# Expert combine: one load for the first tile, and the order of two issues on ScalarE's queue

## The chip, the cores and the metric

The kernel runs on one core of one Trainium2 chip. The metric is the device time of one execution in microseconds; lower is better. The profile is of one execution on that core, and its times are counted from the first instruction (the span's start).

## The reference

For each of 16 x 1024 tokens, two experts' outputs of 512 numbers are multiplied by their two weights and added:

```
expert_outputs   [16, 1024, 2, 512] float32
combine_weights  [16, 1024, 2]      float32
out = sum(expert_outputs * combine_weights[..., newaxis], axis=2)   # [16, 1024, 512]
```

In all, 67.1 MB of expert outputs and 0.13 MB of weights are read, and 33.6 MB are written.

## The kernel before

The 16,384 tokens lie over 128 partitions, 128 tokens to each. A token's two expert rows are 4 KB on end, its output 2 KB. The first 115 tokens of each partition (`main`) form one block of the input, the last 13 (`LAST`) another, so that a partition's tokens in a tile are one contiguous row in memory: 13 tokens are 52 KB of input and 26 KB of output.

The tokens go through ten tiles (`TILES`: 13, 13, 12, 13, 13, 13, 12, 13, 13, 13 tokens per partition). The buffer `et` has four rooms (`ROOM`), and tile g uses room g mod 4. Tiles 0 to 3 are loaded at the start, from SyncE's queue (`load`, line 76); `FIRST` gives the sizes of these loads. In the kernel before there are five, as the first tile is cut into 2 and 11 tokens, and the load of the 2 tokens is told to make rows of no more than 4 KB (`max_dma_last_dim`).

`combine` computes in place. For tiles 0 to 7 VectorE multiplies the whole tile by the weights (line 88) and adds the two halves into the room's beginning (line 97). For tile 8 ScalarE does a part (lines 92, 94, 96, 97). Tile 9 goes token by token through ScalarE (line 102) and VectorE (line 103). Each result is stored (line 130) from ScalarE's queue, except the last two stores, which go from SyncE's: that of tiles 7 and 8 together and that of tile 9. When a tile is stored and its store has landed, SyncE loads the tile that uses the room next.

ScalarE's queue issues four small DMAs first: 16 rows of 512 B of zeroes, spread over the output (`ahead`, line 111; the zeroes come from `zt`, which VectorE sets at line 108, and the real output overwrites them later); the weights of the first 115 tokens (`weights`, line 79; 920 B per partition); and the weights of the last 13 in two halves of the partitions (line 114). Then it loads its activation table with a first small activation (line 115).

The order of instructions on each engine is that of the program (`manual_schedule`). The waits between them are put in by the framework, on semaphores; it has eight for DMAs, and a DMA that takes over one of them waits until the DMA that had it has landed. Both queues, SyncE's (q1 in the profile) and ScalarE's (q10), feed the same 16 DMA engines. One row of a transfer is one packet on one engine.

Of the kernel before, what the change touches and what calls it, by code (L numbers as in the profile page):

```python
# [1 line left out]

# [4 lines left out]


@with_exitstack
def kernel(  # L10
    ctx: ExitStack,
    tc: tile.TileContext,
    expert_outputs: bass.AP,
    combine_weights: bass.AP,
    out: bass.AP,
):

    nc = tc.nc
    b, s, k, h = expert_outputs.shape
    assert k == 2
    n = b * s
    P = nc.NUM_PARTITIONS
    per = n // P
    assert per * P == n

    ROOM = [13, 13, 12, 13]
    ROOMS = len(ROOM)  # L30
    SITE = [sum(ROOM[:i]) for i in range(ROOMS)]
    TILES = [13, 13, 12, 13, 13, 13, 12, 13, 13, 13]
    FIRST = [2, 11, 13, 12, 13]
    STORES = [[0], [1], [2], [3], [4], [5], [6], [7, 8], [9]]
    WHOLE = [0, 1, 2, 3, 4, 5, 6, 7]
    MIXED = [8]
    ALONE = 3
    FREE = {9: 0}
    LAST = 13
    assert all(c <= ROOM[g % ROOMS] for g, c in enumerate(TILES))  # L40
    assert sum(TILES) == per and [g for st in STORES for g in st] == list(range(len(TILES)))
    main = per - LAST
    starts = [sum(TILES[:g]) for g in range(len(TILES))]

    def rows(x):

        first = x[0 : P * main, :].rearrange("(p t) f -> p t f", p=P)
        second = x[P * main : n, :].rearrange("(p t) f -> p t f", p=P)
        return lambda t, c: first[:, t : t + c, :] if t < main else second[:, t - main : t - main + c, :]

    flat = out.rearrange("b s h -> (b s) h")
    eo = rows(expert_outputs.rearrange("b s k h -> (b s) (k h)"))
    cw = rows(combine_weights.rearrange("b s k -> (b s) k"))
    o = rows(flat)

    dt = mybir.dt.float32
    mult = mybir.AluOpType.mult
    add = mybir.AluOpType.add
    copy = mybir.ActivationFunctionType.Copy

    pool = ctx.enter_context(tc.tile_pool(name="all", bufs=1))
    et = pool.tile([P, sum(ROOM), k * h], dt)
    halves = et.rearrange("p j (k h) -> p (j k) h", k=k)
    wt = pool.tile([P, per * k], dt)
    wk = wt.rearrange("p (t k) -> p t k", k=k)
    zt = pool.tile([16, 128], dt)
    warm = pool.tile([P, 1], dt)

    def place(t):
        g = max(g for g in range(len(TILES)) if starts[g] <= t)  # L70
        return SITE[g % ROOMS] + t - starts[g]

    def load(t, c, **kw):
        at = place(t)
        assert place(t + c - 1) == at + c - 1
        nc.sync.dma_start(out=et[:, at : at + c], in_=eo(t, c), **kw)  # L76

    def weights(q, t, c):
        q.dma_start(out=wk[:, t : t + c, :], in_=cw(t, c))

    def combine(g, base):
        at, c, t0 = SITE[g % ROOMS], TILES[g], starts[g]
        if g in WHOLE or g in MIXED:
            room = halves[:, k * at : k * (at + c), :]
            x0, x1 = et[:, at : at + c, 0:h], et[:, at : at + c, h : 2 * h]
            if g in WHOLE:
                wb = wt[:, k * t0 : k * (t0 + c)].unsqueeze(2).to_broadcast([P, k * c, h])
                nc.vector.tensor_tensor(out=room, in0=room, in1=wb, op=mult)  # L88
            else:
                for i in range(ALONE, c):  # L90
                    x = et[:, at + i, 0:h]
                    nc.scalar.activation(out=x, in_=x, func=copy, scale=wt[:, k * (t0 + i) : k * (t0 + i) + 1])  # L92
                w1 = wk[:, t0 : t0 + c, 1:2].to_broadcast([P, c, h])
                nc.vector.tensor_tensor(out=x1, in0=x1, in1=w1, op=mult)  # L94
                w0 = wk[:, t0 : t0 + ALONE, 0:1].to_broadcast([P, ALONE, h])
                nc.vector.tensor_tensor(out=x0[:, 0:ALONE], in0=x0[:, 0:ALONE], in1=w0, op=mult)  # L96
            nc.vector.tensor_tensor(out=halves[:, base : base + c, :], in0=x0, in1=x1, op=add)  # L97
            return
        for i in range(c):
            t = k * (t0 + i)  # L100
            x0, x1 = halves[:, k * (at + i), :], halves[:, k * (at + i) + 1, :]
            nc.scalar.activation(out=x0, in_=x0, func=copy, scale=wt[:, t : t + 1])  # L102
            nc.vector.scalar_tensor_tensor(  # L103
                out=halves[:, base + i, :], in0=x1, scalar=wt[:, t + 1 : t + 2], in1=x0, op0=mult, op1=add
            )

    with tc.manual_schedule():
        nc.vector.memset(zt, 0.0)  # L108

        ahead = flat[0 : P * main, :].rearrange("(q t) h -> q (t h)", q=16)  # L110
        nc.scalar.dma_start(out=ahead[:, 0:128], in_=zt)  # L111
        weights(nc.scalar, 0, main)
        for half in (slice(0, P // 2), slice(P // 2, P)):
            nc.scalar.dma_start(out=wk[half, main:per, :], in_=cw(main, per - main)[half])
        nc.scalar.activation(out=warm, in_=nc.const_aps.tensor(1.0, (P, 1), dt), func=copy)  # L115

        t = 0
        for i, c in enumerate(FIRST):
            load(t, c, **({"max_dma_last_dim": k * h * 4} if i == 0 else {}))
            t += c  # L120
        assert t == sum(TILES[:ROOMS])
        for j, st in enumerate(STORES):
            room = FREE.get(st[0], st[0] % ROOMS)
            base, c = SITE[room] * k, 0
            for g in st:
                combine(g, base + c)
                c += TILES[g]
            assert c <= k * ROOM[room]
            q = nc.sync if j in (7, 8) else nc.scalar
            q.dma_start(out=o(starts[st[0]], c), in_=halves[:, base : base + c, :])  # L130
            for g in st:
                if g + ROOMS < len(TILES):
                    load(starts[g + ROOMS], TILES[g + ROOMS])


# [1 line left out]
_INS = ['expert_outputs', 'combine_weights']  # L137
_OUTS = [((16, 1024, 512), 'float32')]


# [23 lines left out]
```

## Time and profile before

| what | value |
|---|---|
| time, median of 3 runs | 238.95 us (238.85 to 239.05) |
| profiled execution, span from first to last instruction | 237.1 us |
| VectorE busy in the span | 190.0 us (80%) |
| ScalarE busy | 15.8 us (7%) |
| moved by DMA | 100.80 MB in 3344 packets, mean 425 GB/s over the span |
| packets of SyncE's queue (q1) | 77.33 MB, 75.9% of the 16 engines' time |
| packets of ScalarE's queue (q10) | 23.47 MB, 23.0% |

The profile gives for the profiled execution its span alone; the runs' times are device times of other executions of the same program and include what lies before and behind the span. In the profile's rows, PE, DVE, ACT, POOL and SP are TensorE, VectorE, ScalarE, GpSimd and SyncE; a q behind a name (SPq, ACTq) is that engine's queue, on which DMAs are issued. `et` is the tile buffer, `wt` the weights, `zt` the zeroes, `out_dram` the output.

### The profile page before, as it was taken

The page shows a single profiled execution, that of the slowest core. Times are in us where ns is not written, and L with a number is a line of the kernel's source. Part 1 is how long each engine was busy: PE and PEld are TensorE (multiplying, and loading weights), DVE is VectorE, ACT ScalarE, POOL GpSimd, SP SyncE. Part 2 cuts the span into 40 slices and gives each one's busy share as a digit, 9 for nine tenths or more (in the row PEclk, how much of TensorE's full clock was granted, in tenths as well). Part 3 has the DMA queues.
Part 4 walks back from the last instruction along what each step waited for, and adds up shares of the span by engine and source line. Part 5 has one row for each costly group of instructions (what it writes and reads, how often), then busy time and mean ns, then how long its engine had stood idle before and what let it go on. Part 6 is the DMA issues. An engine that isn't in the chain of part 4 may idle for free.

```text
span 237.1 us, 154 instructions
## 1 busy us (share of the span) xinstructions
DVE 190.0 (80%) x33; ACT 15.8 (7%) x25; POOL 0.2 (0%) x4
## 2 busy tenths in 40 slices
DVE  0006999999999999999999998998499969919400
ACT  2000000000000000000000000000000055019200
POOL 0000000000000000000000000000000000000000
DMA  8999999989999999999899999999899999899996
GB/s 300 388 481 434 432 421 398 470 348 485 449 431 458 431 440 390 486 420 420 359 492 409 409 509 392 431 503 431 359 431 503 420 397 483 381 431 431 431 431 287
DMA packets 3344, 100.80 MB, mean 425 GB/s; under 512 B 512, under 2 KB 656, under 8 KB 912
## 3 DMA queue, kind: packets, MB, share of 16 engines
q1 hardware_dynamic: 2000, 77.33, 75.9%
q10 hardware_dynamic: 1344, 23.47, 23.0%
HBM read 67.24 MB, written 33.56 MB: 425 GB/s over the span
## 4 chain that ended last, share of the span: by engine, by line
DVE 55%; DMA 36%; issue 1%; ACT 0%; DVEq 0%; ACTq 0%; SPq 0%
DVE et L88 35%; DVE et L97 17%; DMA out_dram<-et 17%; DMA et<-in_expert_outputs_dram 12%; DMA wt<-in_combine_weights_dram 8%; DVE et L103 3%; ACT et L102 0%; DVEq L159 0%; ACTq L111 0%; DVE zt L108 0%; DVEq L88 0%; SPq L76 0%; ACTq L102 0%
## 5 line engine op out<-in xcount | busy, mean ns | idle before, releaser
L88 DVE TENSOR_TENSOR et<-et,wt 128x13312 f32<-128x13312 f32 (+1 forms) x8 | 110.0, 13754 | 23.8 <-DMA wt<-in_combine_weights_dram 18.7
L97 DVE TENSOR_TENSOR et<-et 128x6656 f32<-128x6656 f32 (+1 forms) x9 | 62.8, 6973 | 0.4
L92 ACT ACTIVATE et<-et,wt 128x512 f32<-128x512 f32 x10 | 6.2, 708 | 188.0 <-DMA et<-in_expert_outputs_dram 188.0
L103 DVE SCALAR_TENSOR_TENSOR et<-et,wt 128x512 f32<-128x512 f32 x13 | 8.7, 747 | 5.0 <-ACT et L102 5.0
L102 ACT ACTIVATE et<-et,wt 128x512 f32<-128x512 f32 x13 | 8.1, 707 | 14.0 <-DMA et<-in_expert_outputs_dram 14.0
L94 DVE TENSOR_TENSOR et<-et,wt 128x6656 f32<-128x6656 f32 x1 | 7.1, 7093 | 2.3 <-DMA et<-in_expert_outputs_dram 2.3
L96 DVE TENSOR_TENSOR et<-et,wt 128x1536 f32<-128x1536 f32 x1 | 1.8, 1751 | 0.0
L115 ACT ACT_TABLE_LOAD x1 | 1.3, 1283 | 3.1 <-issue 3.1
L108 DVE MEMSET zt<- 16x128 f32 x1 | 0.2, 165 | 0.8 <-PEq L148 0.8
L115 ACT ACTIVATE warm<-const-float32-1.0 128x1 f32<-128x1 f32 x1 | 0.2, 203 | 0.0
L148 POOL MEMSET const-bfloat16-1.0<- 128x1 bf16 x1 | 0.1, 102 | 0.0
L148 POOL MEMSET const-uint8-127<- 128x1 uint8 x1 | 0.1, 101 | 0.0
L148 POOL MEMSET const-float32-0.0<- 128x1 f32 x1 | 0.1, 99 | 0.2 <-issue 0.2
L148 POOL MEMSET const-float32-1.0<- 128x1 f32 x1 | 0.1, 98 | 0.0
## 6 DMA issues: line engine op xcount, KB each, us to landing
et<-in_expert_outputs_dram SPq DMA_DIRECT2D x7, 6656.0 KB, 32.2
out_dram<-et ACTq DMA_DIRECT2D x5, 3328.0 KB, 34.7
et<-in_expert_outputs_dram SPq DMA_DIRECT2D x2, 6144.0 KB, 41.1
out_dram<-et SPq DMA_DIRECT2D x1, 6656.0 KB, 19.9
out_dram<-et ACTq DMA_DIRECT2D x2, 3072.0 KB, 37.2
et<-in_expert_outputs_dram SPq DMA_DIRECT2D x1, 5632.0 KB, 18.2
out_dram<-et SPq DMA_DIRECT2D x1, 3328.0 KB, 14.0
et<-in_expert_outputs_dram SPq DMA_DIRECT2D x1, 1024.0 KB, 5.0
```

Of the source, the lines that this page charges most:

```text
L88: nc.vector.tensor_tensor(out=room, in0=room, in1=wb, op=mult)
L92: nc.scalar.activation(out=x, in_=x, func=copy, scale=wt[:, k * (t0 + i) : k * (t0 + i) + 1])
L94: nc.vector.tensor_tensor(out=x1, in0=x1, in1=w1, op=mult)
L96: nc.vector.tensor_tensor(out=x0[:, 0:ALONE], in0=x0[:, 0:ALONE], in1=w0, op=mult)
L97: nc.vector.tensor_tensor(out=halves[:, base : base + c, :], in0=x0, in1=x1, op=add)
L102: nc.scalar.activation(out=x0, in_=x0, func=copy, scale=wt[:, t : t + 1])
L103: nc.vector.scalar_tensor_tensor(out=halves[:, base + i, :], in0=x1, scalar=wt[:, t + 1 : t + 2], in1=x0, op0=mult, op1=add)
L108: nc.vector.memset(zt, 0.0)
L115: nc.scalar.activation(out=warm, in_=nc.const_aps.tensor(1.0, (P, 1), dt), func=copy)
L148: nc = _bacc.Bacc("TRN2", target_bir_lowering=False, num_devices=1)
```

## The change

The first tile's 13 tokens are loaded by one DMA, with rows of 52 KB, instead of one of 2 tokens in rows of 4 KB and one of 11 tokens in rows of 44 KB. ScalarE's queue issues the weights of the first 115 tokens first and then the zeroes. In the instruction streams, SyncE has ten loads instead of eleven; ScalarE's first two DMAs change places; the framework's semaphores go round one place earlier, and with them the load of tile 3 takes over the semaphore of the main weights, where it had that of the zeroes. VectorE's instructions are the same, and its first multiply waits for two DMAs instead of three.

```diff
-    FIRST = [2, 11, 13, 12, 13]
+    FIRST = [13, 13, 12, 13]
...
-    def load(t, c, **kw):
+    def load(t, c):
...
-        nc.sync.dma_start(out=et[:, at : at + c], in_=eo(t, c), **kw)
+        nc.sync.dma_start(out=et[:, at : at + c], in_=eo(t, c))
...
+        weights(nc.scalar, 0, main)
         ahead = flat[0 : P * main, :].rearrange("(q t) h -> q (t h)", q=16)
         nc.scalar.dma_start(out=ahead[:, 0:128], in_=zt)
-        weights(nc.scalar, 0, main)
         for half in (slice(0, P // 2), slice(P // 2, P)):
             nc.scalar.dma_start(out=wk[half, main:per, :], in_=cw(main, per - main)[half])
...
-        for i, c in enumerate(FIRST):
-            load(t, c, **({"max_dma_last_dim": k * h * 4} if i == 0 else {}))
+        for c in FIRST:
+            load(t, c)
             t += c
```

## The prediction

> **What bounds the kernel now.** I read the page's totals first, then the stretches of time, to see whether the span is set by VectorE or by the DMA engines.
>
> ```profile
> span 237.1 us, 154 instructions
> DVE 190.0 (80%) x33; ACT 15.8 (7%) x25; POOL 0.2 (0%) x4
> DMA  8999999989999999999899999999899999899996
> DMA packets 3344, 100.80 MB, mean 425 GB/s; under 512 B 512, under 2 KB 656, under 8 KB 912
> DVE 55%; DMA 36%; issue 1%; ACT 0%; DVEq 0%; ACTq 0%; SPq 0%
> ```
>
> VectorE is busy for 80% and the chain gives it the largest share, but the DMA engines have work in every one of the 40 slices. The chain follows one line of releasers, and here it runs through VectorE where two kinds of work run side by side. The stretches (columns: window and length, busy time of DVE, ACT and POOL, clock, DMA share, GB/s) tell them apart:
>
> ```profile
> 0.00:1.80 1.80, 0.17 (x1) 0.00 (x0) 0.20 (x4) 1.00 0.00 0
> 1.80:3.20 1.40, 0.00 (x0) 0.11 (x1) 0.00 (x0) 1.00 0.97 193
> 3.20:4.90 1.70, 0.00 (x0) 1.38 (x2) 0.00 (x0) 1.00 1.01 412
> 5.40:18.90 13.50, 0.00 (x0) 0.00 (x0) 0.00 (x0) 1.00 1.02 438
> ...
> 41.00:49.00 8.00, 8.00 (x1) 0.00 (x0) 0.00 (x0) 1.00 0.98 401
> 49.00:145.00 96.00, 95.41 (x10) 0.00 (x0) 0.00 (x0) 1.00 1.00 433
> 145.00:184.00 39.00, 34.31 (x4) 0.00 (x0) 0.00 (x0) 1.00 1.02 441
> 184.00:213.00 29.00, 22.18 (x4) 6.43 (x11) 0.00 (x0) 1.00 1.00 432
> ...
> 235.70:237.10 1.40, 0.00 (x0) 0.00 (x0) 0.00 (x0) 1.00 0.00 0
> DMA packets 66, 0.27 MB, mean 193 GB/s; under 512 B 0, under 2 KB 0, under 8 KB 66
> ```
>
> The last row is the DMA view of 1.8 to 3.2 us. A packet is counted where it starts, so a short window of large packets is coarse; the 96 us window is not. From 49 us on, the rate is 432 to 441 GB/s whether VectorE is gapless (49 to 145) or not (145 to 213). That is a full pipe: 100.80 MB at 433 GB/s is 232.8 us. Before the first packet lie 1.8 us, behind the last 1.4. These make 236.0; the other 1.1 of the 237.1 are two stretches where the pipe runs below its rate, the start and the stretch from 41 us where the first store joins. At the start, 1.8 to 4.9 us moved 0.27 + 0.70 = 0.97 MB (193 x 1.40 and 412 x 1.70) where 433 GB/s would have moved 1.34: a loss of 0.86 us.
>
> So the end moves only if the first packet starts at another time, if the start loses more or less than 0.86 us, if bytes or packets cost more or less, or if the pipe runs dry. The runs' median is 238.95, which is 1.85 us above the profiled span; I make the sum on the span and add 1.85.
>
> **The change part by part.** The operations that it touches, from the timeline, the DMA issues (size, time to landing) and SyncE's own waits:
>
> ```profile
> 0.73 0.44 SPq L76 DMA_DIRECT2D et<-in_expert_outputs_dram  x1
> 0.81 0.17 DVE L108 MEMSET zt<- 16x128 f32 x1 [0.81 <-PEq L148]
> 1.01 0.39 ACTq L111 DMA_DIRECT2D out_dram<-zt  x1
> 1.43 0.45 ACTq L79 DMA_DIRECT2D wt<-in_combine_weights_dram  x1
> 19.73 14.02 DVE L88 TENSOR_TENSOR et<-et,wt 128x13312 f32<-128x13312 f32 x1 [18.75 <-DMA wt<-in_combine_weights_dram]
> et<-in_expert_outputs_dram SPq DMA_DIRECT2D x1, 5632.0 KB, 18.2
> et<-in_expert_outputs_dram SPq DMA_DIRECT2D x1, 1024.0 KB, 5.0
> wt<-in_combine_weights_dram ACTq DMA_DIRECT2D x1, 115.0 KB, 18.2
> wt<-in_combine_weights_dram ACTq DMA_DIRECT2D x2, 6.5 KB, 31.0
> out_dram<-zt ACTq DMA_DIRECT2D x1, 8.0 KB, 3.9
> et<-in_expert_outputs_dram SPq DMA_DIRECT2D x1, 6144.0 KB, 50.9
> SPq L76 <- DMA out_dram<-zt: 2.1, 1, 2.1
> q10 hardware_dynamic: 113, 0.10, 2.2%
> ```
>
> *One DMA for the first tile.* The 1024 KB that went as 256 packets of 4 KB now go inside 128 packets of 52 KB. At 412 GB/s (the 4 KB stretch once it has settled) 1.05 MB take 2.55 us, at 433 they take 2.42: a gain of 0.1 us, on the path, because the pipe never stops afterwards. The large packets also meet the slow stretch at 1.8 to 3.2 us, which no row shows for them. Bounds: if it is caused by the small packets, up to the whole 0.86 us goes; if each engine's first large row waits once more as long, 0.86 us is added. I take it as unchanged, since in 1.4 us the 16 engines start only 66 packets, four each, and then settle at 412 with the same packets: that looks like a wait for the first data and not like a cost per packet. One issue of 0.44 us leaves SyncE's queue; nothing waited for it (its successors wait behind tile 0's bytes), so it counts nothing.
>
> [...]
>
> *Weights first on ScalarE's queue.* The weights no longer stand behind the zeroes, which wait for the memset that ends at 0.98; they are issued about when SyncE issues tile 0, at 0.73 instead of 1.43. Their packets cost the DMA engines 2.2% of 13.2 us = 0.29 us (the q10 row is for 5.4 to 18.6 us; 112 of its 113 packets are the weights') wherever they run; if some fall into the slow 1.4 us they are free. So 0 to -0.29; I take -0.05, near the end where they still alternate with tile 0's packets, because now both queues begin together and only those ahead of the first data are free. Against it, two issues at once may delay tile 0's first packet: SyncE's issues take 327 to 643 ns (all eleven; then those of the first two loads; then those of tiles 1 and 2; each with the first and last start),
>
> ```profile
> L76 SPq DMA_DIRECT2D et<-in_expert_outputs_dram x11: 327/328/643, 0.7 to 183.9; - x11
> ...
> L76 SPq DMA_DIRECT2D et<-in_expert_outputs_dram x2: 437/449/461, 0.7 to 1.2; - x2
> ...
> L76 SPq DMA_DIRECT2D et<-in_expert_outputs_dram x2: 424/534/643, 1.7 to 2.2; - x2
> ```
>
> and the first took 437, so -0.11 to +0.21; I take 0.
>
> *When VectorE starts.* Before, tile 0 landed at 1.2 + 18.2 = 19.4 us and the weights at 1.43 + 18.2 = 19.6. Its 6.82 MB at 433 GB/s are 15.7 us, and 1.8 + 0.86 + 15.7 + 0.29 = 18.7, so some 0.7 us pass until the last bytes are seen. After, the same sum less the 0.1 and 0.05 above gives 19.3. The weights land a little before it, or, if their packets get in only behind tile 0's first ones, up to one 52 KB round later: 53,248 B x 16 at 433 GB/s = 1.97 us, so 21.3. So VectorE's first multiply starts between 19.4 and 21.4 instead of 19.73.
>
> [...]
>
> That start is covered at both ends:
>
> ```profile
> 54.85 7.09 DVE L97 TENSOR_TENSOR et<-et 128x6656 f32<-128x6656 f32 x1
> 61.97 0.34 ACTq L130 DMA_DIRECT2D out_dram<-et  x1
> 67.80 0.33 SPq L76 DMA_DIRECT2D et<-in_expert_outputs_dram  x1
> 145.69 12.96 DVE L88 TENSOR_TENSOR et<-et,wt 128x12288 f32<-128x12288 f32 x1 [1.10 <-DMA et<-in_expert_outputs_dram]
> 169.18 14.03 DVE L88 TENSOR_TENSOR et<-et,wt 128x13312 f32<-128x13312 f32 x1 [3.94 <-DMA et<-in_expert_outputs_dram]
> 192.63 7.09 DVE L94 TENSOR_TENSOR et<-et,wt 128x6656 f32<-128x6656 f32 x1 [2.30 <-DMA et<-in_expert_outputs_dram]
> 208.61 14.02 SPq L130 DMA_DIRECT2D out_dram<-et  x2
> out_dram<-et SPq DMA_DIRECT2D x1, 6656.0 KB, 19.9
> ```
>
> The second store is issued at 61.97, yet the first has landed only at about 67.8, when SyncE is released to load tile 4: the store queue has 5.8 us of backlog by then, and a start that is 2 us late only lets loads that are queued anyway take the pipe first. Later VectorE waits for loads, 1.10 + 3.94 + 2.30 us. At the end the last store is issued at 208.61 + 14.02 = 222.6 while the one before lands at 228.5: 5.9 us of cover. So a start 1.7 us late costs nothing, and one 0.3 us early brings nothing.
>
> *Zeroes and last weights later.* The zeroes follow the weights' packets, so they land near 21 to 25 us instead of 4.9. The first store, which must wait for them, is issued when VectorE ends tile 0, 19.73 + 14.02 + 7.09 = 40.8: 15 us of cover. The last 13 tokens' weights move back with them by two turns, 3.9 us; they are needed for tile 9, near 212. SyncE waited 2.1 us for the zeroes before it issued tile 3's load, with nothing behind it that could run; it will now wait for the weights, whose semaphore that load takes over, to 19 to 21 us. Tile 2's load, queued ahead, lands only near 53 (2.2 + 50.9), so 30 us of cover remain.
>
> Sum: -0.1 (4 KB rows) - 0.05 (weights) + 0 = -0.15. Span 236.95, time 238.8.
>
> **Rivals.**
>
> *Faster, the start's loss goes.* Large packets bring the pipe to 433 GB/s at once: -0.86 - 0.05, so 238.0. For it: 193 GB/s is only ever seen with the small packets. Against it: some wait for the first data must stay. 11%. Beside it stands, at 2%, a fixed cost per DMA: the time from the first issue to the first packet, 0.73 to 1.8 = 1.1 us, is paid by each load at the head, and one less saves it: 237.7. [...]
>
> *Slower, a cold row costs more.* Each engine's first 52 KB row stalls the pipe a second time, as the first store's arrival does between 41 and 49 us (401 against 433 GB/s, 0.6 us), or SyncE's issue beside ScalarE's starts 0.2 late: +0.6 to +0.86 + 0.2 - 0.15, so 239.4 to 239.9, most likely 239.6. It decides once the start loses 1.5 us instead of 0.86. For it: the trace has no large packet in a cold pipe. 15%.
>
> *Slower, VectorE's late start reaches the end.* The weights land one round late, and that 1.7 us passes through 125 us of gapless VectorE work to the last store: 240.5. It decides where the covers above (5.8 us at the second store, 5.9 at the last) are smaller than the delay; they are three times as large. 7%.
>
> *The change does not do what it says.* The weights gain no ground on tile 0's packets and land with them or behind. I give that even odds; it leaves the forecast as it is and is inside it.
>
> **How the numbers follow.** No change that can be told is within 0.2%, 0.48 us, about what a measurement of this kernel can distinguish: 238.47 to 239.43. The forecast of 238.8 has 63%. Faster: 11 + 2 and 2 for other gains, 15%. Slower: 15 + 7 = 22%. For the range, 238.2 leaves out most of the first rival, 239.9 the late start and the worst of the cold row, together about 17%.
>
> **What would show it.** Right: the first packet at 1.8 us and the rate over 49 to 145 us at 433 again; VectorE's first multiply between 19.4 and 21.4 with no trace of it at the end; the last store's issue some 6 us before the store ahead of it lands; VectorE waiting for loads again, with the sum of those waits near 7 us less its late start. Wrong: a first packet later than 2.1 us or under 0.9 MB moved by 4.9 us (cold row), over 1.2 MB (first rival), a window after 20 us in which the DMA share falls below 0.95, or a tail longer than 1.4 us.

## The result, and the profile after

The changed kernel takes 240.92 us (median; 240.79 to 241.01), the kernel before 238.88 in the same session (238.85 to 239.05). The ratio is 1.0081, 95% interval 1.0068 to 1.0094: slower by 0.8%, outside the forecast's range. Medians of the kernel before in the other sessions lie between 238.88 and 238.90.

The page of the changed kernel, the lines that answer to those of before:

```profile
span 239.2 us, 153 instructions
DVE 190.1 (79%) x33; ACT 15.8 (7%) x25; POOL 0.2 (0%) x4
DMA  7999999999989999999999999989999999999993
DMA packets 3072, 100.80 MB, mean 422 GB/s; under 512 B 496, under 2 KB 640, under 8 KB 640
DMA 63%; DVE 30%; ACT 0%; DVEq 0%; issue 0%; SPq 0%; ACTq 0%
```

The last slice of the DMA line fell from 6 to 3: the span has grown by 2.0 us, and in its last 6 us the DMA engines do little. The stretches of the changed kernel:

```profile
49.00:145.00 96.00, 94.45 (x10) 0.00 (x0) 0.00 (x0) 1.00 1.00 433
145.00:184.00 39.00, 33.77 (x4) 0.00 (x0) 0.00 (x0) 1.00 1.02 442
184.00:213.00 29.00, 24.10 (x5) 6.24 (x10) 0.00 (x0) 1.00 1.00 432
```

These are the rates of before (433, 441, 432). The bytes are the same and the pipe ran at the same rate, so by the mean it should have been done at the same time. It was, but for one of the 16 DMA engines. The DMA view of the last microseconds, first the kernel before (235.0 to 237.1 us), then the changed one (235.3 to 237.95 and 236.3 to 237.95):

```profile
DMA packets 16, 0.00 MB, mean 0 GB/s; under 512 B 16, under 2 KB 16, under 8 KB 16
```

```profile
DMA packets 18, 0.05 MB, mean 20 GB/s; under 512 B 16, under 2 KB 16, under 8 KB 16
...
DMA packets 2, 0.03 MB, mean 16 GB/s; under 512 B 1, under 2 KB 1, under 8 KB 1
```

In the first line all that is left are 16 small packets, the engines' reports that their share of the last store is done: all engines start their last 26 KB row before 235.0. In the changed kernel two rows of 26 KB (0.05 MB) still start after 235.3, and from 236.3 on only one row and one report are left. One engine works alone.

It was late from the start. The DMA view of the first packets, the kernel before from 1.7 to 2.1 us, then the changed kernel from 1.7 to 2.6 and from 2.6 to 4.3:

```profile
DMA packets 17, 0.07 MB, mean 174 GB/s; under 512 B 0, under 2 KB 0, under 8 KB 17
```

```profile
DMA packets 15, 0.80 MB, mean 887 GB/s; under 512 B 0, under 2 KB 0, under 8 KB 0
...
DMA packets 1, 0.05 MB, mean 31 GB/s; under 512 B 0, under 2 KB 0, under 8 KB 0
```

Before, 17 packets of 4 KB start within 0.4 us of each other. After, 15 engines start their first 52 KB row by 2.5 us and one only at 3.4. The packets can be followed, as on one engine the next starts when the one before ends (the late engine's last two rows: 235.96 to 236.94 and 236.94 to 237.93): the row that starts at 3.40 ends at 5.37, the median of the 16 first rows at 4.56, and that engine stays 0.8 us behind through tile 0.

A DMA has landed when the last engine has reported (in the changed kernel the last report of the first store comes at 69.24 us, and SyncE, which waits for that store, issues its next load at 69.32), and the trace keeps the 16 reports of each. I call the time from the median report to the last one the lag. From these records of the one profiled execution of each kernel, in us:

| kernel | lag, tile 0's load | lag, tile 2's load (near 53 us) | lag, tile 3's load (near 77 us) | last store: median report | last store: lag |
|---|---|---|---|---|---|
| before | 0.17 | 0.32 | 0.25 | 236.11 | 0.22 |
| after | 0.80 | 1.59 | 2.16 | 236.14 | 2.13 |

The median engine ends at the same time to 0.03 us. Of the 2.0 us that the span grew, 1.9 are the lag. Of the 16 reports of the last store, 15 come between 235.99 and 236.57 us and one at 238.28. The lag stayed at 2.13 to 2.17 from tile 3's load to the end, so no engine that was ahead took over rows of the late one.

The timeline and waits of the changed kernel show every landing as late as that engine (the row at 69.32 is of SyncE's queue alone; the last four are DMA issues with their time to landing):

```profile
0.72 0.41 ACTq L79 DMA_DIRECT2D wt<-in_combine_weights_dram  x1
1.18 0.44 ACTq L112 DMA_DIRECT2D out_dram<-zt  x1
20.05 14.03 DVE L88 TENSOR_TENSOR et<-et,wt 128x13312 f32<-128x13312 f32 x1 [19.07 <-DMA wt<-in_combine_weights_dram]
...
69.32 0.33 SPq L76 DMA_DIRECT2D et<-in_expert_outputs_dram  x1
...
147.62 12.96 DVE L88 TENSOR_TENSOR et<-et,wt 128x12288 f32<-128x12288 f32 x1 [1.24 <-DMA et<-in_expert_outputs_dram]
171.12 14.03 DVE L88 TENSOR_TENSOR et<-et,wt 128x13312 f32<-128x13312 f32 x1 [3.96 <-DMA et<-in_expert_outputs_dram]
210.45 14.13 SPq L130 DMA_DIRECT2D out_dram<-et  x2
...
out_dram<-et SPq DMA_DIRECT2D x1, 6656.0 KB, 20.0
wt<-in_combine_weights_dram ACTq DMA_DIRECT2D x1, 115.0 KB, 19.3
wt<-in_combine_weights_dram ACTq DMA_DIRECT2D x2, 6.5 KB, 35.5
out_dram<-zt ACTq DMA_DIRECT2D x1, 8.0 KB, 22.6
```

SyncE is released to load tile 4 at 69.32 instead of 67.80, and VectorE's first multiplies of tiles 6 and 7 start 1.93 and 1.94 us later than before.

### The profile page after: what moved, and what is told of

It reads as the page before. It is cut to its first block, busy times and chain, and to the rows that moved or that the text cites. A ratio compares the mean times of both kernels' runs of the same rounds, so it can differ in the third digit from the quotient of the medians.

```text
span 239.2 us, 153 instructions
## 1 busy us (share of the span) xinstructions
DVE 190.1 (79%) x33; ACT 15.8 (7%) x25; POOL 0.2 (0%) x4
## 4 chain that ended last, share of the span: by engine, by line
DMA 63%; DVE 30%; ACT 0%; DVEq 0%; issue 0%; SPq 0%; ACTq 0%
DMA out_dram<-et 29%; DMA et<-in_expert_outputs_dram 25%; DVE et L88 18%; DVE et L97 9%; DMA wt<-in_combine_weights_dram 8%; DVE et L103 3%; ACT et L102 0%; DVEq L159 0%; SPq L76 0%; DVEq L88 0%; ACTq L102 0%
## 6 DMA issues: line engine op xcount, KB each, us to landing
wt<-in_combine_weights_dram ACTq DMA_DIRECT2D x1, 115.0 KB, 19.3
```

## The experiments

The theory after the result: long rows in a cold pipe, that is, at the start of the stream, make one engine late (rows). Its rivals: the order on ScalarE's queue does it, because both queues now start together or because the zeroes come late (order). Each kernel below was timed beside the kernel before; its ratio to it and the 95% interval follow the median. Lags are of one execution, the profiled one, and executions differ: of the kernel before, one of all 62 took 240.72 us (it was not profiled), and the others at most 239.32.

**The order alone.**

```diff
 (before)
+        weights(nc.scalar, 0, main)
         ahead = ...
         nc.scalar.dma_start(out=ahead[:, 0:128], in_=zt)
-        weights(nc.scalar, 0, main)
```

> The kernel before with the new order alone: the main weights issued first, then the zeroes; the first tile is still cut into 2 tokens in 4 KB rows and 11 tokens. In the changed kernel 15 of 16 DMA engines end as before (near 236 us) and one ends 2 us later. Theory rows (large rows in a cold pipe make one engine late): 238.9, no late engine. Theory order (both queues starting together make one engine late, or zeroes that come at 20 us make the first store's stall longer): 240.9, one engine 2 us late at the end. If both halves are needed: 238.9 here and in the run with one load alone.

Measured: 239.54 us (238.81 to 239.91), 1.0024 (1.0015 to 1.0034). Lag 0.52 at tile 0, 0.61 at the end; median engine at 236.1. The order costs some 0.6 us by itself and brings no engine to 2 us. Both theories were half wrong: the order isn't free.

**One load alone.**

```diff
 (before)
-    FIRST = [2, 11, 13, 12, 13]
+    FIRST = [13, 13, 12, 13]
...
-            load(t, c, **({"max_dma_last_dim": k * h * 4} if i == 0 else {}))
+            load(t, c)
```

> The kernel before with the one load of 13 tokens in 52 KB rows alone; zeroes first, then weights, as before. Theory rows: 240.9, with one engine's first row starting near 3.4 us instead of 1.8 to 2.5 and the same engine 2 us late at the end. Theory order: 238.8 and no late engine.

Measured: 241.93 us (241.08 to 242.57), 1.0114 (1.0084 to 1.0144). Lag 0.87 at tile 0, 2.1 near 76 us, 1.9 at the end (the last engine but one 1.05): the late engine is there without the new order. Its first row started at 2.33 us and not at 3.4, but took 3.15 us where later 52 KB rows take 1.97. In all four profiles whose stream begins with 52 KB rows (these two, the run without zeroes and one with the last weights moved), the lag at tile 0 is there when the first rows end: the slowest ends 0.62 to 0.91 us after the median. The median time is also 1.0 above that of the changed kernel. In the profiled execution the zeroes now take turns with 52 KB rows ahead of the weights (timeline, DMA issues and stretches of this run):

```profile
25.96 14.02 DVE L88 TENSOR_TENSOR et<-et,wt 128x13312 f32<-128x13312 f32 x1 [24.98 <-DMA wt<-in_combine_weights_dram]
...
wt<-in_combine_weights_dram ACTq DMA_DIRECT2D x1, 115.0 KB, 24.4
...
75.00:80.00 5.00, 5.00 (x1) 0.00 (x0) 0.00 (x0) 1.00 1.04 437
80.00:95.00 15.00, 14.96 (x3) 0.00 (x0) 0.00 (x0) 1.00 1.01 403
```

VectorE starts 6.2 us later than before and the first store lands late, so tile 4's load is issued at 75.95 instead of 67.80, and no load row starts between 72.4 and 80.2 us. The stores fill the pipe meanwhile (437 GB/s), but when loads and stores join again, the 52 KB rows take 2.15 us on average instead of 1.97, and from 80 to 95 us the rate is 403. The median engine ends at 237.95 instead of 236.1. So within the change the order repairs part of what the one load does: with one load, weights first is worth 241.93 - 240.92 = 1.0 us by the medians. The four executions lie apart, though (241.08, 241.35, 242.51, 242.57), and the profile is of one of the two slow ones; by the others it is 0.2 to 0.4.

**The whole first tile in 4 KB rows.** The changed kernel with `load(t, c, max_dma_last_dim=k * h * 4)` for the first load.

> The changed kernel (one load, weights first) with the whole first tile in 4 KB rows: 1664 packets instead of 128. Theory rows: the late engine is gone; the 4 KB rows cost 412 against 433 GB/s over 6.8 MB, 0.8 us, less what the start loses: 238.9 + 0.7 = 239.6. Theory order: 240.9 + 0.7 = 241.6 with a late engine.

Measured: 239.93 us (239.83 to 240.09), 1.0042 (1.0027 to 1.0057). The time is near the 239.6 of theory rows, but the late engine isn't gone: the lag at tile 0 is 0.75, about that of the changed kernel, though the rows are short and 16 packets had started by 2.14 us. The lag stays, however: 0.77 near 54 and 78 us, 0.83 at the end. So lateness at the start and its growth are two things. The median engine ends at 236.5, 0.4 late; I put that down to the 1664 packets, which no other run tests.

**No zeroes.** The changed kernel without `zt`, its memset and its DMA.

> The changed kernel without the zeroes and their memset; the output is the same, as the zeroes are overwritten. The late engine of the changed kernel loses some 0.5 to 0.8 us at the start and 1.0 us more between 43 and 54 us, when the first store joins. Theory late zeroes (zeroes issued early spare the first store a wait; late ones do so less): without any the loss at the first store is as large or larger, on more engines, 241 to 243. Theory rows: 240.9, since the zeroes have no part in it.

Measured: 240.82 us (240.01 to 240.96), 1.0072 (1.0055 to 1.0089); lag 0.60, 1.40, 2.09, 2.08 at the four places of the table. As the changed kernel (three of four executions; the fourth took 240.01): late zeroes aren't the cause.

**Row lengths between.** Three runs change the first load's rows, with the weights first in all: 2 tokens as one row of 8 KB (`FIRST = [2, 11, 13, 12, 13]` in the changed kernel), and the one load of 13 tokens with its rows limited to 26 KB and to 13 KB (`max_dma_last_dim`).

> The changed kernel (weights first) with its first tile cut into 2 and 11 tokens again, without the limit on the row: the first load has 8 KB rows, 8 per DMA engine. Against the order alone (4 KB rows, 239.5) and one load (52 KB rows, 240.9). Theory row size (what makes one engine late is the length of the first rows): near 239.5, last engine 0.5 to 0.7 us behind the median. Theory one load (that the first load is the whole tile): also near 239.5. If 8 KB is already too long: 240.5 to 241, last engine 2 us behind.

> The changed kernel with the first load's rows limited to 26 KB: 256 packets, 16 per DMA engine, the number of packets that the kernel before has in its first load. Theory row length: a row of 26 KB is half as bad as one of 52 KB or as bad, 240 to 241, last engine 1 to 2 us behind. Theory packet count (16 packets in the first load suffice): 238.8 to 239.2.

> The changed kernel with the first load's rows limited to 13 KB: 512 packets. With 8 KB rows in the first load (2 tokens, same order) the time was 239.1 and the last engine 0.4 us behind the median. Theory row length: 239.1 to 239.6, last engine under 0.8 behind. If what matters is that the whole first tile is one load: 240.9.

| first load | time, us | ratio | lag at tile 0 | tile 2 | tile 3 | last store |
|---|---|---|---|---|---|---|
| 2 tokens, 4 KB rows (the order alone) | 239.54 | 1.0024 (1.0015 to 1.0034) | 0.52 | 0.52 | 0.56 | 0.61 |
| 2 tokens, 8 KB rows | 239.07 | 1.0016 (0.9998 to 1.0034) | 0.42 | 0.43 | 0.47 | 0.46 |
| 13 tokens, 4 KB rows | 239.93 | 1.0042 (1.0027 to 1.0057) | 0.75 | 0.77 | 0.77 | 0.83 |
| 13 tokens, 13 KB rows | 240.18 | 1.0055 (1.0032 to 1.0079) | 0.39 | 0.44 | 0.49 | 0.68 |
| 13 tokens, 26 KB rows | 240.04 | 1.0047 (1.0030 to 1.0063) | 0.88 | 2.11 | 2.50 | 2.46 |
| 13 tokens, 52 KB rows (after) | 240.92 | 1.0081 (1.0068 to 1.0094) | 0.80 | 1.59 | 2.16 | 2.13 |

The packet count isn't it: 16 packets of 26 KB on each engine are as bad at tile 0 as 8 of 52 KB. Nor is row length shown to be it: 4 KB rows for 13 tokens lag more than 13 KB rows. With 13 and 26 KB the executions differ among themselves (239.22 to 241.23 and 239.97 to 241.24) with medians that are alike, and the profile is of one of them: near the low end for 13 KB (239.43), at the high end for 26 KB (241.24). With 8 KB one of ten took 241.19. By these times an engine ends up 2 us late in some executions and not in others, while the changed kernel's five all lie within 240.79 to 241.01. What does order the medians is the rival that the expectations call one load: with weights first, all four runs with one load of 13 tokens take 239.9 us or more, and both with 2 and 11 tokens 239.6 or less. Whether the one load or its rows make the difference stays open.

**A late engine on purpose.** To see whether lateness, whatever its origin, grows, the kernel before got 17 small rows behind its first load:

```diff
 (before, in the loop over FIRST)
             load(t, c, ...)
+            if i == 0:
+                extra = expert_outputs.rearrange("b s k h -> (b s) (k h)")[0:17, 0:300]
+                nc.sync.dma_start(out=et[0:17, SITE[3], 0:300], in_=extra)
```

> The kernel before with one more small load behind its first one: 17 rows of 1,200 B, which tile 3 overwrites later. A transfer of 17 rows should not split evenly over 16 DMA engines; if it goes through one of them, that engine gets 17 small packets, some 0.8 us of work, and is 0.8 us late from 6 us on, whatever the first rows are. Theory lag grows (a DMA engine that is 0.8 us late when the first store joins loses over 1 us more there): last engine 2 us behind at the end, 240.7. Theory lag stays (lateness only adds up): last engine 0.8 behind, 239.5. If the rows spread over all engines: 238.9.

Measured: 240.32 us (239.84 to 241.05), 1.0063 (1.0043 to 1.0082). In the profiled execution one engine alone became late: lag 0.94 at tile 0, with the next engine at 0.16, so the 17 rows did not spread over all engines. The lag then grew to 2.14 at tile 2's load and 2.41 at tile 3's, though the first rows were of 4 KB and the order that of before; the rest of the engines ended on time. The last 2 us of this run (236.3 to 238.2) hold one data row and one report, as in the changed kernel:

```profile
DMA packets 2, 0.03 MB, mean 14 GB/s; under 512 B 1, under 2 KB 1, under 8 KB 1
```

The profiled execution is the slowest of the four (241.05). The others took 239.84 to 240.40; if they were as late at first, their lag grew less. So 17 small rows that make one engine late are enough for 1.4 us by the medians.

**Where the lag grows.** It grows between 43 and 79 us, from where the first store joins the loads. There the 48 KB rows of all engines, else 1.815 us, take longer: those that start from 42 to 46 us together 0.39 us per engine before, 0.37 after. I call this the stall. With 13 tokens in 4 KB rows it was 0.01, and the lag did not grow. Followed packet by packet, the late engine loses more, in rows of its own: with the late engine on purpose, its 48 KB rows from 44.78 and 51.13 us took 2.58 and 2.51 us; in the changed kernel, those from 44.30 and 47.84 us took 2.56 and 2.22. Theories: ScalarE's small DMAs, which take turns with large rows until shortly before (recent), or any first store (cold store).

> The kernel before with 5 tokens instead of 2 in 4 KB rows (5 + 8 for the first tile). In the run with the whole first tile in 4 KB rows the stall of the loads at the first store (0.3 to 0.4 us per DMA engine at 42 to 46 us in the other kernels) was absent, and ScalarE's small DMAs had all landed by 9 us instead of near 37. Theory recent (the stall comes from small DMAs that alternate with large rows until shortly before the first store): they land by 12 us here, no stall, 238.9 - 0.4 + 0.1 = 238.6. Theory cold store (any first store stalls): 239.0 with the stall.

> The changed kernel with the two loads of the last 13 tokens' weights moved from ScalarE's queue to SyncE's, behind tile 3's load; nothing stands on ScalarE's queue between 23 us and the first store. In the changed kernel the late engine is 0.8 us behind the median until 41 us and 2.15 from 79 us on. Theory recent: no stall at the first store, the lag stays 0.8, 239.5. Theory cold store: as the changed kernel, 240.9.

> The kernel before with the same move of the last weights to SyncE's queue. Theory recent: no stall at the first store, 238.5. Theory cold store: 238.9, stall of 0.4 us per engine as before.

With `FIRST = [5, 8, 13, 12, 13]` in the kernel before, the small DMAs land by 10 us. Measured: 239.27 us (238.88 to 241.08), 1.0031 (1.0006 to 1.0056). The stall is 0.19 us per engine, and three of ten executions lie near 241; the profiled one (238.88, the fastest) has no late engine. The one execution of the kernel before that took 240.72 us was among the 21 timed beside this run.

Moving the two last loads of weights behind tile 3's load on SyncE's queue gave 242.00 us on the changed kernel, 1.0152 (1.0110 to 1.0193), and 244.25 on the kernel before, 1.0220 (1.0204 to 1.0235). The stall stayed (0.70 and 0.60 us per engine) with nothing small on ScalarE's queue from 24 us on, which speaks against theory recent. The times don't tell the theories apart, because the move made a new fault: from 76.8 us on, ten small packets on each engine in SyncE's queue take turns with the stores' rows. In the kernel before, tile 4's first rows start 3.9 us later (80.8 instead of 76.9) and the tile lands 5.3 us later (105.3 instead of 100.0); loads run late from there to the end, where the pipe runs dry. The stretch of the kernel before with that move:

```profile
213.00:217.60 4.60, 3.64 (x1) 0.29 (x1) 0.00 (x0) 1.00 0.38 162
```

Two things are seen in the changed kernel with the move. Ahead of the fault the lag grew little, from 0.90 at tile 0 to 1.18 at tile 3's load, though the stall was the longest. And where the pipe ran dry the lag vanished: 0.07 at the last store.

With the late engine on purpose and small DMAs that are done by 10 us, and with the zeroes put into all 128 rows that the first store writes (`nc.scalar.dma_start(out=o(0, 1)[:, 0, 0:128], in_=zt)`), alone and together:

> The kernel before with 5 tokens in 4 KB rows (239.3 in the run of that alone, with several executions near 241) and with the zeroes put into the first 512 B of all 128 rows that the first store writes, instead of 16 rows spread over the output. Theory cold rows (the loads' stall at the first store comes from output rows that nothing has written yet): no stall at 42 to 46 us, no execution near 241, 238.6. Theory other cause: as that run, 239.0 to 239.3 with a stall of 0.2 us per engine.

> The kernel before with 5 tokens in 4 KB rows and the 17 small rows behind the first load, which make one DMA engine 0.75 us late by themselves. Here ScalarE's small DMAs are done by 10 us, so that nothing alternates with the large rows until the first store. Theory lag grows at the first store: last engine 2.1 to 2.4 us behind from 79 us on, 240.5 to 241. If the growth needs the small DMAs of ScalarE's queue: lag stays 0.75, 239.5.

> The run with 5 tokens in 4 KB rows and 17 small rows, and the zeroes in all 128 rows of the first store. Theory cold rows: the lag of 0.75 does not grow, 239.4. Theory other cause: it grows as without them, 240.5 to 241.

| on 5 tokens in 4 KB rows | time, us | ratio | lag at tile 0 | tile 2 | tile 3 | last store |
|---|---|---|---|---|---|---|
| late engine | 240.83 (240.49 to 240.96) | 1.0077 (1.0062 to 1.0092) | 1.01 | 2.14 | 2.15 | 2.19 |
| zeroes in 128 rows | 239.23 (238.97 to 239.41) | 1.0010 (1.0001 to 1.0019) | 0.21 | 0.25 | 0.27 | 0.28 |
| both | 240.57 (240.11 to 241.01) | 1.0074 (1.0057 to 1.0091) | 0.99 | 0.95 | 0.94 | 0.89 |

The small DMAs aren't needed: the lag grows without them. With zeroes in all rows no execution of ten came near 241, and the stall was 0.09 us per engine, but the time stayed at 239.23 where the theory of cold rows expected 238.6. With both, the lag did not grow in the profiled execution (240.11, the fastest), but others reached 241.01, the median of 240.57 is what the other theory expected (240.5 to 241), and the median engine ended 0.5 us later than before. So the runs don't decide whether output rows that nothing has written yet are the cause: why a late engine gets later at the first store stays open. No version here beats the kernel before.

## Why the prediction was wrong

The step that failed is the first one, "the end moves only if" with its list of four. It treats 16 engines as one pipe with a mean rate. The pipe did what was forecast: 433 GB/s, first packet at 1.74 us, median engine done at 236.14 against 236.11. But the end is the last engine's, and the list lacks the case that one engine falls behind. The term that was left at nothing is the start loss, "unchanged" and one number for all engines: one engine lost 0.8 us more than the median in its first row, and 1.4 more where the first store joined. That a late engine by itself makes the time longer is shown by the two runs that make one late with 17 small rows (240.32 and 240.83 us); what makes one late at the start of the changed kernel, and why it then gets later, stays open. Two things could have warned: the first packets' starts are spread over 0.25 us already before; and a start loss taken as a mean says nothing on its spread.

Point by point. *The gain of 0.15 us*: it came and was lost. The median engine was 0.20 us ahead of before at tile 0 (19.05 against 19.25) and 0.18 at tile 1 (34.89 against 35.07), and level at tile 3 (76.42 against 76.39), behind the first store. *The unchanged start loss*: right for the mean, wrong for one engine by 0.8 us at tile 0, which the first store turned into 2.1. *The cold row rival* (239.6, 15%) was the nearest in kind, a large row in a cold pipe, but priced for all engines and at a third of the size (239.6 is 0.7 above the kernel before, the result 2.0). *A fixed cost per DMA* (2%): no run shows its 1.1 us; one load less brought nothing at the end, 236.14 against 236.11 us for the median engine. *Weights*: they took turns behind tile 0's rows and landed at 20.0 us, 0.2 behind tile 0, so they gained no ground, the case given even odds; VectorE started at 20.05, inside 19.4 to 21.4. *That start is covered*: borne out, as stores, loads and the tail kept their order, with 230.45 - 224.58 = 5.9 us of cover at the end again (210.45 + 20.0 against 210.45 + 14.13). But the cover has a limit: in the run with one load alone, VectorE started 6.2 us late, more than the 5.8 us of backlog, and the median engine ended 1.8 us later. *Zeroes near 21 to 25 us*: 1.18 + 22.6 = 23.8. *Last weights two turns later*: 41.1 instead of 37.1, so 4.0 us, two 52 KB rows of 1.97; harmless, as said. *Order*: priced at -0.05; alone, with the split load, it costs 0.6, and the lag of 0.52 in that run says where.

The stretch from 41 to 49 us was also misread. Its 401 GB/s was taken for a loss of 0.6 us, but the run without any stall there shows 393 in the same stretch:

```profile
41.00:49.00 8.00, 8.00 (x2) 0.00 (x0) 0.00 (x0) 1.00 0.91 393
```

Packets are counted where they start, and 8 us hold four or five rows on each engine. The loss read from the rows' own durations is 0.39 us. The sum could have told: 0.86 + 0.6 us is more than the 1.1 us that it left for both stretches.

## What to carry to other kernels

When the DMA engines are the bound, ask for the last engine and not for the mean rate: count the packets in the last microseconds, and see when each engine's first row starts and ends. What one engine lost at the start was still there at the end as long as the pipe never ran dry, here for over 200 us (a lag of 0.80 us at tile 0 and of 2.13 at the last store). Short first rows are no sure remedy: in the old order, 2 or 5 tokens in 4 KB rows kept the lag at tile 0 at 0.17 to 0.34 us where one load in 52 KB rows had 0.87, but with the weights first, 13 tokens in 4 KB rows had 0.75. Put a small transfer that is needed early ahead of long rows, for here it took one turn for each of its packets: the main weights landed 4.6 us after their issue beside 4 KB rows (the order alone) and 19.3 beside 52 KB rows (after). And take more than one profile: the lag differs between executions of one kernel.

## What was not expected of the hardware

Lateness of one engine grew by 1.4 to 1.5 us where stores first joined loads (from 0.80 to 2.16 after; from 0.94 to 2.41 with a late engine on purpose), and in the changed kernel it then stayed constant to 0.05 us for 150 us. The queues took turns row by row, even where a row is 52 KB: in the run with one load alone the weights landed 5.8 us later than in the changed kernel (25.86 against 20.02), three turns of 1.97 us, two of them for the zeroes' one packet and its report on each engine, and one because ScalarE's first packet got in a row later (6.28 against 4.34). In these traces a turn held one row, of 920 B for the weights: in the kernel before, 112 rows of SyncE's queue and 113 of ScalarE's start between 5.4 and 18.6 us. Small packets are costly there in another way than in bytes: with ten of them on each engine in SyncE's queue, ahead of 6.8 MB of load, that load landed 5.3 us later.
